# Projecting the first three channel chunks from x that has not been normalised yet, with x, weights and vectors laid out by the host

## The chip, the core and the metric

One NeuronCore of a Trainium2 chip runs the whole kernel. The metric is the device time of one execution in microseconds (us), the median of three runs. The engines are named as in the profile: PE (matrix products, with PEld for its weight loads), DVE (vector), ACT (scalar functions), POOL (GpSimd) and SP, which only issues DMAs here. Every engine works through its own instructions in the order in which the program holds them.

## What is computed

One layer over 1024 tokens with 1024 channels, all float32:

```
hn   = x * rsqrt(mean(x^2) + eps) * ln_g            # per token
proj = hn @ w_in + b_in                             # 1024 -> 3584 columns = 28 chunks of 128
glu_a, glu_b, z_conv, q, k, v, z_att = split(proj)  # 7 parts of 512 columns = 4 chunks each
u    = glu_a * sigmoid(glu_b)                       # then a convolution over tokens, 31 taps per channel
y_conv = pointwise(silu(layernorm(conv(u))))        # 512 x 512 product
y_att  = attention(q, k, v)                         # 8 heads, windows of a 16 x 64 token grid
out  = rms_norm(x + concat(norm(y_conv) * silu(z_conv), norm(y_att) * silu(z_att)) @ w_out) * final_g
```

Every factor of a matrix product is split into a rounded part and a remainder (`hi`, `lo` for the activations, `wh`, `wl` for the weights), and each product is three matmuls: hi.wh, lo.wh and hi.wl.

## The kernel before

**A planned order.** The function `block` runs on the host and writes the order of all engines by hand. A class `Clock` (L86 to 145) keeps a planned time for PE and for the queues of ACT, DVE and POOL, with a cost per instruction. The work is written as generators ("streams") with a rank. `weave` takes the first stream in rank order that is due, lets it emit instructions until it waits for a planned time, and goes on. A matmul moves the planned time forward. Two kinds of filler stand beside the streams: the taps of the convolution go to DVE whenever DVE's planned queue is empty to within 0.1 us, and the remainders `wl` of the weights go to POOL in the same way. The order is fixed once the program is built: where the chip is slower than the plan, the engines wait for each other in the planned order.

**Buffers.** `Ring` counts free buffers. `r_u` counts a pool of sixteen 4 KB-per-partition buffers in SBUF (the function `U`), which serve x, the tiles of `u`, q, k and v of a head pair, the attention outputs `ya`, and the pointwise weights. A stream that needs one takes it from `r_u` or polls until one is put back. Of the eight PSUM banks, tags `pj`, `s` and `tr` have two each and `o` and `ln` one each.

**The start.** SP loads the eight tiles of 128 tokens x 1024 channels (`xload`, L204), the weights of the first chunk after four of them, then small tensors. Per token tile, `x_tile` (L259) lets ACT (or DVE for tiles 4 and 6) square x and sum it, POOL makes 1/rms of the sum with two instructions (`rs`), and DVE scales the tile in place. `turned` (L279) lets PE transpose the scaled tiles in blocks of 128 x 128 (64 transposes, tile `px`) into PSUM banks of one channel block by 512 tokens; ACT copies each bank to `hi` with the scale `ln_g`, and `low` (L306) lets DVE write `lo` from the bank, the scale and `hi`. Tokens go in two halves, h = 0 and h = 1, of 512 each. The per-channel vectors and the taps arrive in rows and are turned by PE as well.

**The projection.** `prefetch` (L337) loads one weight chunk of 512 KB at a time on SP in 512-byte pieces (one raw buffer, `r_raw`), ACT writes `wh` in two halves, POOL writes `wl` in two halves; two chunks can be held (`r_w`). `proj` (L368) is 8 channel blocks x 3 matmuls of 512 columns into one bank, for one chunk and one token half. The stream `lead` runs `glu` for the pairs g0, g1, g2 (chunk b, then chunk a), then q0, k0 and v0; after it `attention` starts with rank 1 and `fill` (the rest of the projection) with rank 5. In `glu` (L505) a bank of chunk b leaves by ACT as a tanh (tile `sg`), one of chunk a by ACT with its bias, and DVE multiplies both (`glu_out`). When both halves are done, 31 taps for the chunk are queued as filler for DVE. For j = 0 the order is b h0, a h0, b h1, a h1; for j = 1 it is b h0, b h1, a h0, a h1.

**What else matters here.** `bias_rows` (L397) builds the bias of the attention through DRAM with some hundred small DMAs on SP, one per step of other work; attention starts when the first of it is there. Attention walks 32 blocks (4 head pairs of 8). A pair needs q (2 buffers), kh and kl (4), vt (1, put back when v is made) and v (2). `v_out` (L609) makes v; `head_out` takes one buffer for `ya` when a pair is done. `scores` gives back three buffers at the last block of a head. `pw_load` takes two buffers, and two more later, for the pointwise weights; then `pointwise` runs eight tiles of 128 tokens, each also waiting for its taps. Gates (`pz`), the last gates and the output projection (`out`) follow.

The change touches the start (`xload`, `x_tile`, `turned`, `low`, `tap_cols`), `prefetch`, `low_weight`, `proj`, `glu`, `glu_out` and the inputs that the host prepares.

Of the kernel before, what the change touches and what calls it, by code (L numbers as in the profile page):

```python
# [9 lines left out]
F32 = mybir.dt.float32  # L10
# [7 lines left out]
P = 128  # L18
# [35 lines left out]
TURN = 0.02  # L54
QI = 0.1
LW = 10.9
SQ_DVE = (4,6)

# [89 lines left out]
@with_exitstack  # L148
def block(ctx: ExitStack, tc: tile.TileContext, x, vecs, w_in, dw_w, pw_w, pw_b, rpb, w_out, final_g, out):
    nc = tc.nc  # L150
# [14 lines left out]
    ring = lambda n: Ring(ck, n)  # L165
    r_u, r_raw, r_w, r_x, r_uh, r_ul, r_gz, r_y = ring(16), ring(1), ring(2), ring(XB), ring(1), ring(0), ring(1), ring(1)
    r_pt, r_os = ring(2), ring(2)
# [5 lines left out]
    def U(name, dt=F32, shape=(P, 1024)):  # L173
        return big.tile(list(shape), dt, tag="u", name=name)
# [25 lines left out]
    acc = yp.tile([P, NC4, T], F32, name="acc")  # L200
    xt = [U(f"x{t}") for t in range(NT)]

    def xload(t):
        nc.sync.dma_start(out=xt[t], in_=x2[t * P:(t + 1) * P, :])  # L204

# [4 lines left out]
    def wraw(n):  # L210
        c = order[n]
        raw = wrp.tile([P, NK, P], F32, tag="wr", name=f"wr{c}")
        nc.sync.dma_start(out=raw, in_=w_in[0][:, c * P:(c + 1) * P].rearrange("(k p) n -> p k n", p=P))
        return raw

    def wtiles(n):
        c = order[n]
        return (whp.tile([P, NK, P], F32R, tag="wh", name=f"wh{c}"),
                wlp.tile([P, NK, P], F32R, tag="wl", name=f"wl{c}"))

    for t in range(4):
        xload(t)
    raw0 = wraw(0)
    for t in range(4, NT):
        xload(t)
    land = [4.5, 5.9, 7.4, 8.9, 11.8, 13.3, 14.7, 16.2]
    land_w = LW

    vec = half_tile("uh", "vec")[:V_N, :P]
    nc.scalar.dma_start(out=vec, in_=vecs)  # L230
    dwr = half_tile("ul", "dwr")[:TAPS, :C]
    nc.sync.dma_start(out=dwr, in_=dw_w[0])
    pwb = const.tile([P, C], F32, name="pwb")
    nc.sync.dma_start(out=pwb, in_=pw_b[0].partition_broadcast(P))

    cols = const.tile([P, V_N], F32, name="cols")
    pv = bank("tr", "pv")
    nc.tensor.transpose(out=pv[:, :V_N], in_=vec, identity=ident[:V_N, :V_N])
    nc.vector.tensor_copy(out=cols, in_=pv[:, :V_N])
# [4 lines left out]
    dwc = const.tile([P, NC4, 32], F32, name="dwc")  # L244

    def tap_cols():
        yield 19.0
        yield from r_tr.get()
        pd = bank("tr", "pd")
        for c in range(NC4):  # L250
            ck.tp(pd[:, c * 32:c * 32 + TAPS], dwr[:, c * P:(c + 1) * P], ident[:TAPS, :TAPS])
        t = ck.dve("tensor_scalar", out=dwc[:, :, :TAPS],
                   in0=pd[:, :NC4 * 32].rearrange("p (c k) -> p c k", k=32)[:, :, :TAPS], scalar1=0.5, scalar2=None,
                   op0=ALU.mult)
        r_tr.put(t)
        r_ul.put(t)
# [4 lines left out]
    x_ready, hn_ready = {}, {}  # L261

    def x_tile(t):
        yield land[t]
        ss = sm.tile([P, 1], F32, tag="ss", name=f"ss{t}")
        rs = sm.tile([P, 1], F32, tag="rs", name=f"rs{t}")
        eng = "dve" if t in SQ_DVE else "act"
        while t >= 4 and ck.q[eng] > ck.now + QI:
            yield ck.now + 0.1
        if t in SQ_DVE:  # L270
            e = ck.dve("scalar_tensor_tensor", out=acc[:, t % 4, :], in0=xt[t], scalar=1.0 / 1024.0, in1=xt[t],
                       op0=ALU.mult, op1=ALU.mult, accum_out=ss)
        else:
            e = ck.act(out=acc[:, t % 4, :], in_=xt[t], func=AF.Square, scale=1.0 / 32.0, accum_out=ss)
        yield e
        ck.gps("tensor_scalar", 0.2, e, out=rs, in0=ss, scalar1=EPS, scalar2=None, op0=ALU.add)
        e = ck.gps("tensor_tensor", 0.47, 0.0, out=rs, in0=rs, in1=mhalf[:, :1], op=ALU.pow)
        yield e
        x_ready[t] = ck.dve("tensor_scalar", e, 0.55, out=xt[t], in0=xt[t], scalar1=rs, scalar2=None, op0=ALU.mult)  # L279

    def turned(h):

        todo_ = list(range(NK))
        for group in ((("tr", "tr", "s", "s", "o", "ln"),) if h == 0 else ()) + (("tr",), ("s",)) * NK:
            ks, todo_ = todo_[:len(group)], todo_[len(group):]
            pts = []
            for k, tag in zip(ks, group):
                yield from RB[tag].get()
                pts.append((k, tag, bank(tag, f"px{h}_{k}", NB[tag])))
            for j in range(4):  # L290
                t = 4 * h + j
                while t not in x_ready:
                    yield ck.now + 0.1
                if x_ready[t] + ck.HOP > ck.now:
                    yield x_ready[t] + ck.HOP
                for k, tag, pt in pts:
                    ck.tp(pt[:, j * P:(j + 1) * P], xt[t][:, k * P:(k + 1) * P], ident)
                    if j == 3:
                        sl = slice(512 * h, 512 * h + 512)
                        e = ck.act(out=hi[k][:, sl], in_=pt, func=AF.Copy, scale=col(V_LN + k))  # L300
                        ck.spawn(low(h, k, pt, sl, e, RB[tag]), -1)
            yield
        for _ in range(4):
            r_u.put()

    def all_turned():  # L306
        for h in range(2):
            yield from turned(h)

    def low(h, k, pt, sl, t, r):  # L310
        yield t
        t = ck.dve("scalar_tensor_tensor", t, out=lo[k][:, sl], in0=pt, scalar=col(V_LN + k),
                   in1=hi[k][:, sl].bitcast(F32), op0=ALU.mult, op1=ALU.subtract)
        r.put(t)
        hn_ready[k, h] = t

    bias = []
# [6 lines left out]
    for b in sum(prob, []):  # L324
        nc.gpsimd.memset(b, 0.0)
    ck.q["pool"] = 5.0

# [9 lines left out]
    def prefetch():  # L337
        for n in range(len(order)):
            if n < W_AHEAD or "pw" in state:
                yield from r_raw.get()  # L340
                raw, end = (wraw(n), ck.now + 4.0) if n else (raw0, land_w)
                yield from r_w.get()
            else:
                yield from r_w.get()
                yield from r_raw.get()
                raw, end = wraw(n), ck.now + 4.0
            whi, wlo = wtiles(n)
            yield end
            for k0 in range(0, NK, KS):
                kk = slice(k0, k0 + KS)  # L350
                t = ck.act(out=whi[:, kk, :], in_=raw[:, kk, :], func=AF.Copy)
# [15 lines left out]

    def proj(w, h, name, order=None, tag="pj"):  # L368

# [9 lines left out]
        for k in range(NK):  # L379
            while (k, h) not in hn_ready or k >= len(wt):  # L380
                yield ck.now + 0.1
            if max(hn_ready[k, h], wt[k]) > ck.now:
                yield max(hn_ready[k, h], wt[k])
            ck.mm(pj, whi[:, k, :], tok(hi[k]), k == 0, False)
# [122 lines left out]
    def glu(j):  # L507
# [3 lines left out]
        for e, h in ((0, 0), (1, 0), (0, 1), (1, 1)) if j == 0 else ((0, 0), (0, 1), (1, 0), (1, 1)):  # L511
            c = (CH_B, CH_A)[e] + j
            ws[e] = yield from weight(c)
            pj, sl = yield from proj(ws[e], h, f"p{'ba'[e]}{j}_{h}")
            if e == 0:
                yield from r_x.get()
                sgs[h] = X(f"sg{j}_{h}")
                t = ck.act(out=sgs[h], in_=pj, func=AF.Tanh, scale=0.5, bias=hcol(V_BIN + c))
                r_pj.put(t)
            else:  # L520
                t = ck.act(out=uj[:, sl], in_=pj, func=AF.Identity, bias=col(V_BIN + c))
                r_pj.put(t)
                ck.spawn(glu_out(j, h, uj, sgs[h], t), -1)
            if h:
                r_w.put()
            yield

    def glu_out(j, h, uj, sg, t):
        yield t
# [454 lines left out]

    del r_u.free[8:]
    ck.taps = all_taps()
    for t in range(NT):
        ck.spawn(x_tile(t), -2 if t < 4 else 1)
    ck.spawn(all_turned(), 0)
    ck.spawn(tap_cols(), -1)  # L990
    ck.spawn(prefetch(), -1)
# [223 lines left out]
_VECS = ["ln_g", "b_in", "dw_b", "cln_g", "cln_b", "gn_conv_g", "gn_att_g"]  # L1215
_INS = ["x", "vecs", "w_in", "dw_w", "pw_w", "pw_b", "rpb", "w_out", "final_g"]

# [18 lines left out]
```

## Time and profile before

| | |
|---|---|
| median of 3 runs | 571.23 us (568.81 to 573.75) |
| profiled execution | 572.21 us |
| its span in the trace | 570.4 us |
| PE busy | 539.3 us, 95% of the span |
| DVE busy | 412.2 us, 72% |
| mean granted clock | 0.992 |

The span leaves 1.8 us of the execution's time outside. Rows of the trace are listed below; in them L127 is every matmul, L131 every transpose on PE, L136 every ACT, L140 every DVE and L144 every POOL instruction that the planner emits, so tiles tell them apart.

### The profile page before, as it was taken

To read this page: it belongs to the slowest core of one execution; us is meant where nothing else is said; L and a number is where in the kernel's file an instruction comes from. 1 tells how busy PE (TensorE), PEld (TensorE's weight loads), DVE (VectorE), ACT (ScalarE), POOL (GpSimd) and SP (SyncE) were. 2 spreads that over 40 slices of the span, in tenths; PEclk is the share of its full clock that TensorE was granted. 3 is DMA by queue.
4 is the path that set the end of the run, shared out by engine and by line. 5 is a ranking of instruction groups with operands and counts; after the bars stand their busy time and mean duration, and the time that the engine had idled before them with its cause. 6 is when DMAs were issued, how large, how long until landed. Compare 5 with 4: busy or idle time off the path is not lost.

```text
span 570.4 us, 7827 instructions
## 1 busy us (share of the span) xinstructions
PE 539.3 (95%) x2717; PEld 447.2 (78%) x2717; DVE 412.2 (72%) x665; ACT 260.1 (46%) x634; POOL 195.1 (34%) x176
## 2 busy tenths in 40 slices
PE   4999999898999998999997999999999999999995
PEld 3688888676888886888786788788888888888885
DVE  4747999987999979988999884667564365464232
ACT  6552221124555153655465645875665555253121
POOL 7513543232222343232525152542515552031121
PEclk9999999998999999999998999999999999999999
DMA  9413546663123442263241241101101470044221
GB/s 330 145 14 84 168 128 223 172 192 111 40 57 103 125 105 66 74 149 103 65 142 54 77 120 46 38 26 52 39 0 38 158 284 0 2 148 145 78 75 74
DMA packets 62331, 57.74 MB, mean 101 GB/s; under 512 B 9981, under 2 KB 51765, under 8 KB 62292
## 3 DMA queue, kind: packets, MB, share of 16 engines
q1 hardware_dynamic: 62222, 57.22, 33.6%
q8 instruction: 21, 0.34, 0.3%
q14 instruction: 18, 0.15, 0.1%
q10 hardware_dynamic: 70, 0.03, 0.0%
HBM read 36.58 MB, written 11.58 MB: 84 GB/s over the span
## 4 chain that ended last, share of the span: by engine, by line
PE 71%; DVE 17%; DMA 4%; issue 3%; ACT 2%; SPq 2%; POOL 1%; POOLq 0%; ACTq 0%; DVEq 0%
PE out L127 15%; PE pz L127 13%; DVE acc L140 12%; PE pv L127 6%; PE pk L127 6%; PE pq L127 5%; PE po L127 4%; PE pw L127 4%; PE pb L127 4%; PE ptp L131 3%; PE pa L127 3%; PE s L127 3%; DMA kl<-kl 1%; PE po L131 1%; DMA x<-in_x 1%
## 5 line engine op out<-in xcount | busy, mean ns | idle before, releaser
L140 DVE SCALAR_TENSOR_TENSOR acc<-glu,dwc,acc 128x512 f32<-128x512 f32 (+25 forms) x150 | 186.7, 1270 | 1.2
L144 POOL TENSOR_TENSOR wl<-wr,wh 128x512 fp32r<-128x512 f32 x56 | 93.9, 1695 | 153.0 <-ACT wh L136 147.7
L127 PE MATMUL pz<-hi,wh 128*128 128x512 f32 x128 | 52.2, 408 | 0.0
L127 PE MATMUL out<-wol,yh 128*128 128x512 f32 (+1 forms) x136 | 51.2, 377 | 0.0
L127 PE MATMUL out<-woh,yl 128*128 128x512 f32 (+1 forms) x136 | 51.2, 377 | 0.0
L127 PE MATMUL out<-woh,yh 128*128 128x512 f32 (+1 forms) x136 | 51.2, 377 | 0.0
L127 PE MATMUL pz<-hi,wl 128*128 128x512 f32 x128 | 50.3, 393 | 0.1
L127 PE MATMUL pz<-lo,wh 128*128 128x512 f32 x128 | 50.1, 391 | 0.0
L136 ACT ACTIVATE wh<-wr 128x512 fp32r<-128x512 f32 x56 | 32.3, 628 | 30.5 <-DMA wr<-in_w_in 20.9
L140 DVE TENSOR_TENSOR ptl<-ptp,pth 128x512 fp32r<-128x512 f32 x64 | 37.0, 614 | 1.2 <-ACT pth L136 1.2
L136 ACT ACTIVATE pth<-ptp 128x512 fp32r<-128x512 f32 x64 | 31.8, 543 | 13.2 <-PE ptp L131 12.4
L140 DVE CUSTOM_DVE_ANT_0 s<-s,bias 128x264 f32<-128x264 f32 (+1 forms) x64 | 30.2, 512 | 7.3 <-PE s L127 4.2
L140 DVE TENSOR_TENSOR xr<-out,xr 128x512 f32<-128x512 f32 (+1 forms) x17 | 11.1, 660 | 33.6 <-PE out L127 29.1
L136 ACT ACTIVATE prob<-s,mx 128x264 f32<-128x264 f32 (+1 forms) x64 | 33.6, 536 | 0.6 <-DVE mx L140 0.4
L136 ACT ACTIVATE os<-po 128x256 f32<-128x256 f32 x32 | 12.4, 387 | 41.9 <-PE po L127 41.8
L131 PE MATMUL ptp<-ident,prob 128*128 128x128 f32 x224 | 30.0, 273 | 0.0
L127 PE MATMUL pq<-hi,wh 128*128 128x512 f32 x64 | 26.6, 416 | 3.2 <-DVE v L140 3.2
L127 PE MATMUL po<-pth,v 128*128 128x256 f32 x112 | 29.5, 291 | 0.0
L144 POOL TENSOR_TENSOR ams<-ams,mhalf 128x8 f32<-128x8 f32 x8 | 14.6, 1819 | 43.5 <-DVE ams L140 43.5
L127 PE MATMUL po<-ptl,v 128*128 128x256 f32 x112 | 29.3, 290 | 0.0
L127 PEld LDWEIGHTS out<-woh,yh 128*128 128x128 f32 x136 | 25.6, 188 | 4.7
L127 PEld LDWEIGHTS out<-woh,yl 128*128 128x128 f32 x136 | 25.6, 188 | 4.7
(153 smaller groups left out, 1371.0 us busy)
## 6 DMA issues: line engine op xcount, KB each, us to landing
wr<-in_w_in SPq DMA_DIRECT2D x28, 512.0 KB
x<-in_x SPq DMA_DIRECT2D x8, 512.0 KB
wor<-in_w_out SPq DMA_DIRECT2D x8, 512.0 KB
xr<-in_x SPq DMA_DIRECT2D x8, 512.0 KB
out<-xr SPq DMA_DIRECT2D x16, 256.0 KB
kh<-kh SPq DMA_DIRECT2D x24, 128.0 KB
kl<-kl SPq DMA_DIRECT2D x24, 128.0 KB
q<-ql SPq DMA_DIRECT2D x16, 128.0 KB
```

Of the source, the lines that this page charges most:

```text
L127: self.nc.tensor.matmul(out, lhsT=lhsT, rhs=rhs, start=start, stop=stop)
L131: self.nc.tensor.transpose(out=out, in_=in_, identity=identity)
L136: self.nc.scalar.activation(**k)
L140: getattr(self.nc.vector, fn)(**k)
L144: getattr(self.nc.gpsimd, fn)(**k)
```

## The change

The host hands in x twice (by tokens, and by channels as `xt`), the weights in the order chunk, partition, channel block (so 4 KB in a row per partition), and the vectors and taps already by channels. The start then reads x by channels (`xc`, one tile per channel block) in 256 KB pieces, and makes `hi` and `lo` from `xc * ln_g` without 1/rms. The first three chunks (`RAW`: b of pair 0, a of pair 0, b of pair 1), both halves, are projected from these. x by tokens is loaded later, only for the sums of squares; 1/rms is broadcast over the partitions by a PE transpose (`stats`) into `rsb`. The six banks of the three chunks are multiplied by `rsb` on DVE as they leave PSUM, and `normalise` then scales `xc` in place and writes `hi` and `lo` anew for the other 25 chunks. Six buffers of `r_u` are free at the start instead of eight: `xc` has eight, the second raw weight chunk one, `rsb` one. The diff, without the signature, the load-time constants and the parts of `glu` that only move:

```
+RAW = ((0, 0), (1, 0), (0, 1))
-    xt = [U(f"x{t}") for t in range(NT)]
+    xc = [U(f"xc{k}") for k in range(NK)]
+    def xload(k0, n, h):
+        for k in range(k0, k0 + n):
+            nc.sync.dma_start(out=xc[k][:, 512 * h:512 * h + 512], in_=xt[k][:, 512 * h:512 * h + 512])
+    def tload(t):
+        nc.sync.dma_start(out=acc[:, t % 4, :], in_=x2[t * P:(t + 1) * P, :])
...
-        nc.sync.dma_start(out=raw, in_=w_in[0][:, c * P:(c + 1) * P].rearrange("(k p) n -> p k n", p=P))
+        nc.sync.dma_start(out=raw, in_=w_in[c])
...
+    raws0 = [wrp.tile([P, NK, P], F32, tag="wr", name=f"wr{order[0]}"), U(f"wr{order[1]}", F32, (P, NK, P))]
+    for h in range(2):
+        for k in range(NK):
+            first(("x", k, h), 0.25, xload, k, 1, h)
+            if h == 0 and k in (0, 3):
+                first(("w", 0, (k + 1) // 4), 0.25, wload, 0, 4 * (k // 3), 4)
+        if h == 0:
+            first(("w", 1, 0), 0.5, wload, 1, 0, NK)
     for t in range(4):
+        first(("t", t), 0.5, tload, t)
...
+    rsb = U("rsb")
+    def x_raw(k, h):
+        yield land["x", k, h]
+        sl = slice(512 * h, 512 * h + 512)
+        t = ck.act(out=hi[k][:, sl], in_=xc[k][:, sl], func=AF.Copy, scale=col(V_LN + k))
+        yield t
+        raw_ready[k, h] = ck.dve("scalar_tensor_tensor", t, out=lo[k][:, sl], in0=xc[k][:, sl], scalar=col(V_LN + k),
+                                 in1=hi[k][:, sl].bitcast(F32), op0=ALU.mult, op1=ALU.subtract)
+    def stats():
+        for h in range(2):
+            tag = ("o", "ln")[h]
+            yield from RB[tag].get()
+            pb = bank(tag, f"rsb{h}", NB[tag])
+            for j in range(4):
+                t = 4 * h + j
+                yield land["t", t]
...
+                e = ck.act(out=acc[:, j, :], in_=acc[:, j, :], func=AF.Square, scale=1.0 / 32.0, accum_out=ss)
+                if h == 0:
+                    tload(t + 4)
...
+                ck.tp(pb[:, j * P:(j + 1) * P], rs.broadcast_to([P, P]), ident)
+            e = ck.act(out=rsb[:, 512 * h:512 * h + 512], in_=pb, func=AF.Copy)
...
+    def normalise(h):
+        while h not in raw_done or h not in rs_ready:
+            yield ck.now + 0.1
+        yield rs_ready[h]
+        sl = slice(512 * h, 512 * h + 512)
+        for k in range(NK):
+            t = ck.dve("scalar_tensor_tensor", out=xc[k][:, sl], in0=xc[k][:, sl], scalar=col(V_LN + k), in1=rsb[:, sl],
+                       op0=ALU.mult, op1=ALU.mult)
+            ck.spawn(split_x(k, h, sl, t), -1)
+            yield
+    def split_x(k, h, sl, t):
+        yield t
+        t = ck.act(t, out=hi[k][:, sl], in_=xc[k][:, sl], func=AF.Copy)
+        yield t
+        q = dict(out=lo[k][:, sl], in0=xc[k][:, sl], in1=hi[k][:, sl].bitcast(F32), op=ALU.subtract)
+        t = ck.gps("tensor_tensor", 1.4, t, **q) if k % 2 else ck.dve("tensor_tensor", t, **q)
         hn_ready[k, h] = t
+        if h:
+            r_u.put(t)
...
-            r_raw.put(t)
+            (r_u if n == 1 else r_raw).put(t)
...
+            if (e, j) in RAW:
+                tag = ("pj", "s", "tr")[h if j == 0 else 2]
+                pj, sl = yield from proj(ws[e], h, f"p{'ba'[e]}{j}_{h}", None, tag, raw_ready)
+                if (e, j) == RAW[-1]:
+                    raw_done[h] = True
+                ck.spawn((raw_a if e else raw_b)(j, h, c, uj, sgs, pj, sl, RB[tag]), -1)
...
+    def raw_a(j, h, c, uj, sgs, pj, sl, banks):
...
+        t = ck.dve("tensor_tensor", out=uj[:, sl], in0=pj, in1=rsb[:, sl], op=ALU.mult)
+        banks.put(t)
+        yield t
+        t = ck.act(t, out=uj[:, sl], in_=uj[:, sl], func=AF.Identity, bias=col(V_BIN + c))
+        yield from glu_out(j, h, uj, sgs, t)
...
-    del r_u.free[8:]
+    del r_u.free[6:]
```

`raw_b` does the same with tanh for chunk b. `x_tile`, `turned`, `low` and `tap_cols` are gone, and with them the 64 transposes and those of the vectors and taps. `rsb` is never put back to `r_u`.

## Rows read from the trace of the kernel before

**Rows 1.** Page, busy time of the engines over the span.
```profile
PE 539.3 (95%) x2717; PEld 447.2 (78%) x2717; DVE 412.2 (72%) x665; ACT 260.1 (46%) x634; POOL 195.1 (34%) x176
```

**Rows 2.** Stages: from:to, length, busy PE, PEld, DVE, ACT, POOL, granted clock, DMA share, GB/s.
```profile
0.00:46.80 46.80, 37.60 (x173) 29.50 (x174) 24.20 (x34) 23.82 (x40) 22.04 (x41) 1.00 0.50 160
125.60:277.80 152.20, 145.58 (x783) 121.03 (x781) 135.19 (x227) 75.25 (x196) 45.30 (x25) 0.99 0.35 93
277.80:307.50 29.70, 26.68 (x152) 22.75 (x152) 28.43 (x54) 16.05 (x43) 8.89 (x6) 1.00 0.41 118
307.50:341.90 34.40, 32.18 (x166) 26.88 (x167) 29.50 (x54) 18.86 (x48) 13.57 (x14) 0.95 0.31 80
341.90:447.60 105.70, 104.68 (x584) 88.31 (x584) 60.40 (x134) 66.00 (x175) 44.88 (x40) 1.00 0.11 33
```

**Rows 3.** Chain that ended last, in order of time: start, length, what.
```profile
2.11 7.01 DMA x<-in_x
39.88 5.45 PE pa L127 x24
```

**Rows 4.** Groups of instructions in 0 to 46 us: count, busy, mean ns, idle before.
```profile
L131 PE MATMUL px<-ident,x 128*128 128x128 f32 x64 | 12.5, 345 | 3.9 <-DVE x L140 3.9
```

**Rows 5.** Order of time, PE, 16 to 19 us: start, length, line, what.
```profile
17.46 0.63 PE L127 MATMUL pb<-lo,wh 128*128 128x512 f32 x1
17.88 0.63 PE L127 MATMUL pb<-hi,wl 128*128 128x512 f32 x1
```

**Rows 6.** Order of time, ACT, 55 to 69 us.
```profile
56.24 0.69 ACT L136 ACTIVATE sg<-pb,hcols 128x512 f32<-128x512 f32 x1 [4.75 <-PE pb L127]
67.12 0.69 ACT L136 ACTIVATE glu<-pa,cols 128x512 f32<-128x512 f32 x1 [4.75 <-PE pa L127]
```

**Rows 7.** The chain again, 45 to 73 us.
```profile
56.02 1.28 DVE acc L140
58.64 2.19 DVE acc L140
```

**Rows 8.** Order of time, POOL, 0 to 64 us.
```profile
11.62 3.93 POOL L144 TENSOR_TENSOR wl<-wr,wh 128x512 fp32r<-128x512 f32 x2 [0.19 <-ACT wh L136]
58.13 1.62 POOL L144 TENSOR_TENSOR wl<-wr,wh 128x512 fp32r<-128x512 f32 x1 [5.83 <-ACT wh L136]
```

**Rows 9.** Order of time, DVE, around 14 us and from 260 us.
```profile
14.36 2.72 DVE L140 SCALAR_TENSOR_TENSOR lo<-px,cols,hi 128x512 fp32r<-128x512 f32 x4
...
262.67 0.74 DVE L140 SCALAR_TENSOR_TENSOR acc<-glu,dwc,acc 128x512 f32<-128x512 f32 x1
278.38 0.54 DVE L140 TENSOR_SCALAR acc<-glu,dwc,cols 128x512 f32<-128x512 f32 x1
340.39 1.50 DVE L140 SCALAR_TENSOR_TENSOR acc<-glu,dwc,acc 128x498 f32<-128x498 f32 x2
```

**Rows 10.** Groups of DVE instructions by shape.
```profile
L140 DVE TENSOR_TENSOR xn<-pw,pwb 128x512 f32<-128x512 f32 x8 | 5.5, 692 | 24.4 <-PE pw L127 24.4
L140 DVE TENSOR_TENSOR ul<-xn,uh 128x512 fp32r<-128x512 f32 x8 | 5.5, 683 | 3.2 <-ACT uh L136 3.2
```

**Rows 11.** Stages again, around the stall at 305 us.
```profile
305.00:307.50 2.50, 0.29 (x2) 0.00 (x0) 2.46 (x10) 2.39 (x8) 0.52 (x1) 1.00 0.35 105
307.50:312.00 4.50, 3.97 (x20) 3.67 (x21) 4.40 (x11) 3.04 (x9) 2.88 (x4) 0.62 0.00 0
```

**Rows 12.** Order of time, PE, 265 to 276 us.
```profile
268.99 0.41 PE L127 MATMUL pv<-hi,wl 128*128 128x512 f32 x1
270.66 0.60 PE L131 MATMUL pvt<-ident,vt 128*128 128x128 f32 x4
273.24 1.04 PE L131 MATMUL yat<-ident,ytok 128*128 128x128 f32 x8
274.12 0.60 PE L131 MATMUL pvt<-ident,vt 128*128 128x128 f32 x4
```

**Rows 13.** Order of time, SP's DMA issues, 255 to 310 us.
```profile
295.99 0.37 SPq L826 DMA_DIRECT2D pwr<-in_pw_w  x1
```

More of the change, by code (lines that the diff above doesn't have):

```diff
@@ L243, in block @@
     hcol = lambda r: hcols[:, r:r + 1]
[L244 to L256, printed above, removed]
+    nc.vector.tensor_scalar(out=dwc, in0=dwc, scalar1=0.5, scalar2=None, op0=ALU.mult)
@@ L281, in turned @@
[L281 to L289, printed above, removed]
+    raw_ready, hn_ready, rs_ready, raw_done = {}, {}, {}, {}
+    rsb = U("rsb")
[6 more added lines that the diff above has]
+                                 in1=hi[k][:, sl].bitcast(F32), op0=ALU.mult, op1=ALU.subtract)
@@ L302, in turned @@
-            yield
[L303 to L310, printed above, removed]
+                yield land["t", t]
+                ss = sm.tile([P, 1], F32, tag="ss", name=f"ss{t}")
+                rs = sm.tile([P, 1], F32, tag="rs", name=f"rs{t}")
+                e = ck.act(out=acc[:, j, :], in_=acc[:, j, :], func=AF.Square, scale=1.0 / 32.0, accum_out=ss)
+                if h == 0:
+                    tload(t + 4)
+                    land["t", t + 4] = max(land.get(("t", t + 3), 0.0), e + 3.0) + 1.5
@@ L339, in prefetch @@
             if n < W_AHEAD or "pw" in state:
-                yield from r_raw.get()
-                raw, end = (wraw(n), ck.now + 4.0) if n else (raw0, land_w)
+                if n != 1:
+                    yield from r_raw.get()
+                raw, end = (wraw(n), ck.now + 4.0) if n > 1 else (raws0[n], 0.0)
                 yield from r_w.get()
@@ L379, in proj @@
         for k in range(NK):
-            while (k, h) not in hn_ready or k >= len(wt):
+            while (k, h) not in x_ready or k >= len(wt):
                 yield ck.now + 0.1
-            if max(hn_ready[k, h], wt[k]) > ck.now:
-                yield max(hn_ready[k, h], wt[k])
+            if max(x_ready[k, h], wt[k]) > ck.now:
+                yield max(x_ready[k, h], wt[k])
             ck.mm(pj, whi[:, k, :], tok(hi[k]), k == 0, False)
@@ L526, in glu, with raw_b, glu_out @@
             yield
-    def glu_out(j, h, uj, sg, t):
+    def raw_b(j, h, c, uj, sgs, pj, sl, banks):
+        while h not in rs_ready:
+            yield ck.now + 0.1
+        yield rs_ready[h]
+        yield from r_x.get()
+        sg = X(f"sg{j}_{h}")
+        t = ck.dve("tensor_tensor", out=sg, in0=pj, in1=rsb[:, sl], op=ALU.mult)
+        banks.put(t)
+        yield t
+        ck.act(t, out=sg, in_=sg, func=AF.Tanh, scale=0.5, bias=hcol(V_BIN + c))
+        sgs[h] = sg
+    def raw_a(j, h, c, uj, sgs, pj, sl, banks):
+        while h not in rs_ready:
+            yield ck.now + 0.1
+        yield rs_ready[h]
+        t = ck.dve("tensor_tensor", out=uj[:, sl], in0=pj, in1=rsb[:, sl], op=ALU.mult)
+        banks.put(t)
+        yield t
+        t = ck.act(t, out=uj[:, sl], in_=uj[:, sl], func=AF.Identity, bias=col(V_BIN + c))
+        yield from glu_out(j, h, uj, sgs, t)
+    def glu_out(j, h, uj, sgs, t):
+        while h not in sgs:
+            yield ck.now + 0.1
+        sg = sgs[h]
         yield t
@@ L983, in lead @@
         state["lead"] = True
-    del r_u.free[8:]
+    del r_u.free[6:]
     ck.taps = all_taps()
[L987 to L990, printed above, removed]
+    for h in range(2):
+        for k in range(NK):
+            ck.spawn(x_raw(k, h), -2)
+        ck.spawn(normalise(h), -1)
+    ck.spawn(stats(), -1)
     ck.spawn(prefetch(), -1)
@@ L1224 @@
     nc = bacc.Bacc("TRN2", target_bir_lowering=False, num_devices=1)
-    inputs = dict(inputs, vecs=np.concatenate([np.asarray(inputs[n])[0].reshape(-1, P) for n in _VECS]))
+    a = {n: np.asarray(v) for n, v in inputs.items()}
+    inputs = dict(
+        a,
+        xt=a["x"][0].T.reshape(NK, P, T),
+        vecs=np.concatenate([a[n][0].reshape(-1, P) for n in _VECS]).T,
+        w_in=a["w_in"][0].reshape(NK, P, -1, P).transpose(2, 1, 0, 3),
+        taps=np.pad(a["dw_w"][0], ((0, 1), (0, 0))).reshape(32, NC4, P).transpose(2, 1, 0))
     arrays, args = {}, []
```

99 lines of the change are left out of this document (35 added, 64 removed).

## The prediction

> **What bounds the kernel now.** I read the page's busy times first, then the chain that ended last, then stage windows, then the order of time at the start and wherever the change's buffers and waits come into play. PE is busy for 95% of the span, DVE for 72% [rows 1]: the kernel is bound by PE wherever PE is fed. The windows say where it is not. Up to 46.8 us PE is busy for 37.6 us, but a good part of that is transposes of x and matmuls at half clock: 64 transposes take 12.5 us, with 3.9 us of waiting for the scaled x before them [rows 4]; matmuls start 0.42 us apart at 17.5 us [rows 5], against 5.45 us for a projection of 24, or 0.227 us each, at 40 us [rows 3]. [...] The two token halves of b and a of pair 0 end at 45.3 us; four projections at full pace need 4 x 5.45 = 21.8 us, so the start costs 23.5 us. From 341.9 to 447.6 us PE is busy for 104.7 of 105.7 us [rows 2]; there is nothing to win there but work.
>
> So time gained at the start is kept if later waits don't take it back. Two could. DVE is full from 47 us on: it works 135 of 152 us up to 277.8 us, and 28.4 of the next 29.7 [rows 2], the taps filling what the rest leaves. And the sixteen buffers of `r_u` gate the later stages: the second load of pointwise weights is issued at 295.99 us [rows 13], when the fourth block of a head gives three buffers back.
>
> **The start, step by step.** The change ends the wait for the norm. SP's burst grows from 8 x loads, one weight chunk and three small loads to 16 pieces of x, 3 of weights, 4 tiles of x by tokens and two small loads, about 7.3 MB before the other four x tiles. The first four tiles, 2.1 MB, landed 7.0 us after 2.1 us [rows 3], 300 GB/s with the latency in it. So x of the first half with chunk b (2.6 MB) is there by 2.1 + 8.7 = 10.8 us, and the first four token tiles by 26 us at the latest. DVE's eight `lo` set the pace of the first projection: from about 5.3 us to 14.2 at 1.1 us each, the middle of 0.74 and 1.37 (worked out below). Add the last three matmuls, and it ends at 14.9 us; at the half-clock pace all the way 24 x 0.427 from 5 us give 15.2, so the clock changes little here. Three more projections end at 14.9 + 16.4 = 31.3 us. The eight broadcasts of 1/rms are transposes like those removed, at most 12.5/64 = 0.2 us each: 1 us. So b and a of pair 0 end at 32.2 us and b of pair 1, two more, at 43.1 us. Before, the same point is where ACT takes the second bank of b at 56.24 us [rows 6], so PE is 13 us ahead there. The loads of x by tokens cost nothing, since 1/rms is wanted only when banks run short, at 43 us; the bias DMAs behind them on SP slip by the few microseconds of the four late loads, which attention doesn't see, as `fill` can run until the bias is there.
>
> **The price: `hi` and `lo` a second time.** `normalise(h)` may start when the raw chunks have read that half: at 37.7 us for h = 0. Per half, DVE multiplies a bank (0.69 us [rows 10]), does eight SCALAR_TENSOR_TENSOR on two SBUF operands and four subtractions (0.68 [rows 10]); POOL does four subtractions, ACT eight copies. All eight multiplications are emitted before the first subtraction, so a of pair 1 waits for the ninth instruction.
>
> What one such multiplication takes isn't in the trace; a tap of 512 columns is the nearest, also with two SBUF operands: 0.74 us alone [rows 9]. A tap of 1024 takes 1.28 us alone and 2.19 while POOL writes a `wl` [rows 7], which is there at 58.13 [rows 8]. The factor is 1.71, so 0.74 becomes 1.27, and up to 1.37 with the hops. `lo` from PSUM shows no such loss: four took 2.72 us, 0.68 each [rows 9], while POOL wrote two `wl` [rows 8]; the change moves that operand into SBUF too.
>
> Lower bound, POOL never in the way: 37.7 + 0.7 + 8 x 0.74 + 0.7 = 45.0 us. PE waits 1.9 us and ends the first half of a at 50.4; DVE ends the three other subtractions at 47.0, then the other half's bank, eight multiplications and one subtraction at 54.3; PE waits 3.9 us and ends at 59.7. Upper bound, POOL always in the way and a tap of 2.2 us in front: 51.6, 58.8 (with 1.7 us lost to half clock, below) and 75.5. Before, the point is 66.9 us, just before ACT takes the bank at 67.12 [rows 6]. So the 13 us become anything from a gain of 7.2 to a loss of 8.6 us. POOL has 8 subtractions and two `wl` to do, some 12.7 us at 1.27, against 22 us of DVE work, and so is in the way of about half of it: I take the middle, +0.5 us.
>
> The half clock after a wait: after 2.2 us of idle PE at 305 us the granted clock was 0.62 for 4.5 us [rows 11], so 4.5 x 0.38 = 1.7 us lost. A wait as short as the lower bound's first may cost nothing.
>
> [...]
>
> **What the rest does.** DVE's taps resume at about 62 us instead of running from 46.8 us, and start a little earlier; they are some 13 to 15 us behind. That lies beside PE's work: the first token half of the last chunk has its taps at 278.4 us, the second at 341.9 [rows 9], while the pointwise weights arrive only after 296 us [rows 13] and the last four tiles start far later. If the taps were over 18 us late, this cover would be gone.
>
> `r_u` has fifteen buffers in place of sixteen, as `rsb` keeps one. By my count of takes and puts from the code, all sixteen are held at one place, around 270 us: `u` 1, `ya` 1, q, k and vt of pair 2 7, pointwise 2, q of pair 3 2, v 2, the next `ya` 1. There the trace has the last matmul of v at 268.99, the transposes for v at 270.66 and 274.12, and those for `ya` between them at 273.24 us [rows 12]. With fifteen, `ya` must wait until vt is put back, so it moves from 273.2 to about 275.5, and with it the next pair's first block. PE holds q of pair 3 in the meantime, so the cost is from 0 to 3 us; I take 2. Weights in 4 KB pieces instead of 512 bytes cost or give nothing, as PE never waits for them after the start.
>
> **Sum.** 572.2 (profiled) + 0.5 + 2 = 574.7 us. The profiled execution lay 1.0 us above the median, so 573.7; I say 573.5 us. Its own range is 567 to 580.
>
> **Rivals.**
> 1. *The gain survives.* If POOL's subtractions hardly meet DVE's, the lower bound holds: 571.2 - 7.2 = 564 us if the wait for the buffer is hidden, 566 if it isn't. For it: ACT has to make `hi` before POOL can start, so POOL's work lags. Against it: `wl` of two chunks are due in the same stretch.
> 2. *DVE and POOL in turn.* 18.8 + 12.7 = 31.5 us from 37.7 us end the last `lo` at 69.2 us; with the last matmuls and the half clock after a long wait a ends at about 72 us, 5 us late. With the taps late too, 571.2 + 5 + 2 + 2 = 580 us. It decides from the point at which the wait before the second half of a passes 7 us.
> 3. *The fifteenth buffer locks.* In the order of time on PE, v's takes come about 1 us before `ya`'s (268.99 against 273.24 less some 3.2 us of POOL work and hops). If `ya` takes its buffer first, v gets one and holds it; the next to come free is that of the last `u`, after its taps, at about 312 us when DVE has only taps to do and they are 13 us late. Attention stands for 35 us; PE has the rest of q and one gate, 21 us, and then idles for about 21. Price 16 to 35 us, so about 593 us. It decides from a shift of 1 us between the two.
> 4. *The loads are too slow*, so that x by channels, not DVE, paces the start: 2.6 MB at 300 GB/s ends 3.4 us before DVE does, so little is left for this; time as before.
>
> **How the numbers follow.** Forecast 0.38, first rival 0.30, second 0.17, third 0.13, fourth 0.02. A measurement of this kernel tells about 1%, or 5.7 us, from no change. Faster: 0.29 of the first. Same: 0.35 of the forecast, 0.01 each of the first two rivals, 0.02 of the fourth. Slower: 0.03 of the forecast, 0.16 of the second, 0.13 of the third. The range 561 to 592 leaves out the best of the first rival and the worse part of the third.
>
> **What would show it.** Right: b of pair 1 is through PE by 43 us, with two waits of PE on DVE's `lo` right behind it, 2 to 8 us each, and a of pair 1 ends near 67 us; multiplications near 0.74 us alone and 1.3 us beside POOL; the first taps run for a moment before 38 us and then from about 62 us; `ya` of pair 1 behind the second v transpose. Wrong: a of pair 1 ending before 61 us; attention standing for over 10 us near 270 or 360 us; the pointwise tiles waiting for taps.

## The result, and the profile after

The changed kernel takes 624.49 us (622.14 to 625.09), against 571.88 us (568.81 to 573.75) for the kernel before measured beside it: a ratio of 1.092, with an interval of 1.086 to 1.098. That is slower by 52.6 us and outside the range of the prediction. Pairs are counted from 0 here, as in the prediction. (Some expectations below call the first pair "pair 1": "v of pair 1" that ends the lead is v of pair 0, and pvt "of pair 3" and "of pair 4" are those of pairs 2 and 3.)

The page first, beside [rows 1]: PE's busy time is almost the same, its span is not.

```profile
PE 543.6 (87%) x2656; PEld 448.1 (72%) x2656; DVE 427.5 (69%) x682; ACT 274.4 (44%) x656; POOL 209.2 (34%) x184
```

The same five stages as in [rows 2] (from:to, length, busy PE, PEld, DVE, ACT, POOL, granted clock, DMA share, GB/s). In the fourth PE works 9.76 of 34.4 us, where it had 32.18, and at a granted clock of 0.57.

```profile
0.00:46.80 46.80, 37.68 (x147) 29.68 (x147) 23.60 (x29) 29.13 (x48) 22.78 (x41) 0.96 0.76 250
125.60:277.80 152.20, 149.07 (x790) 124.08 (x789) 138.86 (x227) 72.16 (x188) 44.93 (x24) 0.99 0.35 96
277.80:307.50 29.70, 21.25 (x101) 16.83 (x99) 29.42 (x27) 9.31 (x19) 14.82 (x9) 0.93 0.27 80
307.50:341.90 34.40, 9.76 (x44) 7.72 (x44) 27.58 (x48) 5.06 (x15) 0.00 (x0) 0.57 0.08 25
341.90:447.60 105.70, 99.60 (x552) 83.86 (x553) 57.51 (x135) 67.49 (x179) 39.13 (x38) 0.98 0.19 53
```

PE's waits of the whole run (waiting line, what released it: total, times, longest):

```profile
PE po L126 <- DVE v L139: 29.8, 1, 29.8
PE pa L126 <- DVE lo L139: 11.5, 2, 9.2
...
PE pz L126 <- POOL wl L143: 5.5, 1, 5.5
```

PE in order of time, the ends that the prediction named and the long wait. The lines of before for `yat` and `pvt` are [rows 12].

```profile
25.97 0.32 PE L130 MATMUL rsb<-ident,rs 128*128 128x128 f32 x1 [1.99 <-POOL rs L143]
...
47.90 0.39 PE L126 MATMUL pb<-hi,wl 128*128 128x512 f32 x1
...
55.65 0.27 PE L130 MATMUL rsb<-ident,rs 128*128 128x128 f32 x1
...
68.93 0.79 PE L126 MATMUL pa<-lo,wh 128*128 128x512 f32 x1 [9.16 <-DVE lo L139]
...
76.62 0.39 PE L126 MATMUL pa<-hi,wl 128*128 128x512 f32 x1
...
295.82 1.03 PE L130 MATMUL yat<-ident,ytok 128*128 128x128 f32 x8
296.70 0.60 PE L130 MATMUL pvt<-ident,vt 128*128 128x128 f32 x4
297.60 0.66 PE L130 MATMUL pvt<-ident,vt 128*128 128x128 f32 x4 [0.30 <-DVE ya L139]
298.58 1.17 PE L130 MATMUL ptp<-ident,prob 128*128 128x128 f32 x6 [0.32 <-ACT ya L135]
329.50 0.55 PE L126 MATMUL po<-pth,v 128*128 128x256 f32 x1 [29.75 <-DVE v L139]
```

PE stands for 29.8 us because v of pair 2 isn't written, though its transposes are through PE by about 298 us. DVE in order of time says why, and what the start looks like:

```profile
40.65 8.50 DVE L139 SCALAR_TENSOR_TENSOR xc<-xc,cols,rsb 128x512 f32<-128x512 f32 x8
49.08 0.68 DVE L139 TENSOR_TENSOR sg<-pb,rsb 128x512 f32<-128x512 f32 x1
49.68 4.05 DVE L139 TENSOR_TENSOR lo<-xc,hi 128x512 fp32r<-128x512 f32 x4
56.59 8.99 DVE L139 SCALAR_TENSOR_TENSOR xc<-xc,cols,rsb 128x512 f32<-128x512 f32 x8 [2.86 <-ACT rsb L135]
...
68.06 2.63 DVE L139 TENSOR_TENSOR lo<-xc,hi 128x512 fp32r<-128x512 f32 x4
...
71.92 0.81 DVE L139 TENSOR_SCALAR acc<-glu,dwc,cols 128x1024 f32<-128x1024 f32 x1
...
293.75 3.11 DVE L139 SCALAR_TENSOR_TENSOR acc<-glu,dwc,acc 128x1010 f32<-128x1010 f32 x3
...
303.70 25.31 DVE L139 SCALAR_TENSOR_TENSOR acc<-glu,dwc,acc 128x512 f32<-128x512 f32 x30
328.94 1.41 DVE L139 TENSOR_TENSOR v<-pvt,v 128x256 fp32r<-128x256 f32 x4
```

Thirty taps of the last `u` run back to back, and directly behind them v is written: v had to wait for the buffer that the last `u` gives back. The first tap starts at 71.92 us; before, it was 46.81. The last 1024-wide tap (the end of the third `u`) ends at 296.9 us; before, at 248.1, as the second of two taps that one row of DVE's order of time holds:

```profile
246.16 1.92 DVE L140 SCALAR_TENSOR_TENSOR acc<-glu,dwc,acc 128x510 f32<-128x510 f32 x2
```

ACT and POOL in the start show where 1/rms was late:

```profile
30.49 1.15 ACT L135 ACTIVATE wh<-wr 128x512 fp32r<-128x512 f32 x2 [6.94 <-PE pb L126]
31.55 1.04 ACT L135 ACTIVATE acc<-acc 128x1024 f32<-128x1024 f32 x1
...
37.15 0.60 ACT L135 ACTIVATE rsb<-rsb 128x512 f32<-128x512 f32 x1 [4.47 <-PE rsb L130]
...
55.95 0.60 ACT L135 ACTIVATE rsb<-rsb 128x512 f32<-128x512 f32 x1 [4.41 <-PE rsb L130]
```

```profile
24.60 0.35 POOL L143 TENSOR_SCALAR rp<-rp 120x31 f32<-120x31 f32 x1 [8.12 <-DMA rp<-in_rpb]
25.03 0.23 POOL L143 TENSOR_SCALAR rs<-ss 128x1 f32<-128x1 f32 x1
...
47.19 4.79 POOL L143 TENSOR_TENSOR lo<-xc,hi 128x512 fp32r<-128x512 f32 x3
52.05 0.55 POOL L143 TENSOR_SCALAR rs<-ss 128x1 f32<-128x1 f32 x1
```

The first 1/rms stands on POOL behind `rp`, a small instruction for the bias of the attention that waits 8.12 us for its DMA. The fourth square stands on ACT behind a `wh` that waits 6.94 us for PE to let its buffer go; the last 1/rms stands on POOL behind three subtractions.

### The profile page after: what moved, and what is told of

It is laid out like the page before. It is cut to its first block, busy times and chain, and to the rows that moved or that the text cites. A ratio compares the mean times of both kernels' runs of the same rounds, so it can differ in the third digit from the quotient of the medians.

```text
span 622.9 us, 7800 instructions
## 1 busy us (share of the span) xinstructions
PE 543.6 (87%) x2656; PEld 448.1 (72%) x2656; DVE 427.5 (69%) x682; ACT 274.4 (44%) x656; POOL 209.2 (34%) x184
## 5 line engine op out<-in xcount | busy, mean ns | idle before, releaser
L139 DVE SCALAR_TENSOR_TENSOR acc<-glu,dwc,acc 128x512 f32<-128x512 f32 (+25 forms) x150 | 180.9, 1237 | 1.2
L126 PE MATMUL po<-pth,v 128*128 128x256 f32 x112 | 30.2, 294 | 30.6 <-DVE v L139 29.8
L135 ACT ACTIVATE wh<-wr 128x512 fp32r<-128x512 f32 x56 | 32.3, 628 | 33.4 <-DMA wr<-in_w_in 15.7
L126 PEld LDWEIGHTS po<-pth,v 128*128 128x128 f32 x112 | 21.7, 194 | 32.8 <-issue 30.0
L126 PE MATMUL pa<-lo,wh 128*128 128x512 f32 x64 | 27.0, 423 | 11.5 <-DVE lo L139 11.5
L139 DVE TENSOR_TENSOR ytok<-po,ytok 128x128 f32<-128x128 f32 x32 | 9.2, 288 | 35.6 <-ACT ytok L135 35.0
L126 PE MATMUL pb<-hi,wh 128*128 128x512 f32 x64 | 27.7, 433 | 6.0 <-ACT wh L135 6.0
L126 PEld LDWEIGHTS pz<-hi,wl 128*128 128x128 f32 x128 | 24.6, 192 | 11.4 <-POOL wl L143 5.9
```

The source lines that it names most:

```text
L126: self.nc.tensor.matmul(out, lhsT=lhsT, rhs=rhs, start=start, stop=stop)
L135: self.nc.scalar.activation(**k)
L139: getattr(self.nc.vector, fn)(**k)
```

## The experiments

All medians are beside runs of the kernel before on the same chip (570.96 to 572.12 us). The table holds what decided: the start of the first full run of taps, the end of the last 1024-wide tap, the end of the lead (last matmul of v of pair 0), how many of the 93 wide taps of the first three `u` had not started then, and the start of the second `pvt` of pairs 2 and 3. Times are in us, from the order of time of each trace; where PE's work ends, the start of its last matmul is given. In e9, e10 and e12 the first tap stands alone, some 4 us ahead of the next; in e11 a single tap ran at 45.4 us.

| run | first tap | third u's taps end | lead ends | wide taps left | pvt pair 2 | pvt pair 3 | median |
|---|---|---|---|---|---|---|---|
| before | 46.8 | 248.1 | 125.4 | 42 | 274.1 | 362.0 | 571.88 |
| after | 71.9 | 296.9 | 133.9 | 54 | 297.6 | 407.3 | 624.49 |
| e1, after, 16 buffers | 71.8 | 304.1 | 133.9 | 54 | 276.5 | 390.9 | 598.34 |
| e2, before, 15 buffers | 45.1 | 245.5 | 123.7 | 42 | 296.0 | 389.9 | 609.07 |
| e3, e1 and sums first | 69.7 | 302.6 | 130.3 | 54 | 275.0 | 389.2 | 593.18 |
| e4, e1 with two raw chunks | 70.1 | 279.7 | 141.8 | 47 | 285.3 | 374.3 | 585.65 |
| e5, after, v asks first | 72.4 | 298.0 | 134.8 | 54 | 298.7 | 387.9 | 596.93 |
| e6, before, taps late | 69.2 | 301.2 | 122.9 | 59 | 291.8 | 386.3 | 591.14 |
| e7, e3 and e4 together | 60.5 | 271.7 | 133.0 | 47 | 277.3 | 364.6 | 576.47 |
| e9, e7, lo on DVE | 50.2 | 256.8 | 127.4 | 46 | 269.2 | 357.6 | 569.19 |
| e10, e3, lo on DVE | 61.3 | 296.7 | 125.9 | 54 | 269.1 | 383.2 | 589.83 |
| e11, before, taps 14 us late | 61.6 | 280.3 | 120.9 | 53 | 283.4 | 369.9 | 593.04 |
| e12, e7, order alone | 55.2 | 262.6 | 134.0 | 45 | 275.2 | 362.9 | 572.02 |

**The buffer.** e1 gives `rsb` back after the last of its seven readers; e2 takes one buffer from the kernel before.

```
-    rsb = U("rsb")
+    rsb, rsb_left = U("rsb"), [7]
+    def rsb_read(t):
+        rsb_left[0] -= 1
+        if not rsb_left[0]:
+            r_u.put(t)
```

> The change, with the buffer of rsb put back to r_u after its last reader (16 buffers in the long run instead of 15). Theory A (the lock on the buffers at pair 2 costs most): the wait of 29.8 us of PE on v at 300 us goes, the second load of pointwise weights is issued near 300 us instead of 337, and the time falls by 35 to 45 us, to 580 to 590. Theory B (the taps, some 25 us late, hold the buffer of the second u and make the shortage by themselves): PE still waits over 15 us for v of pair 2 and the time stays above 605.

```
-    del r_u.free[8:]
+    del r_u.free[7:]
```

> The kernel before with one buffer of r_u taken away and nothing else. Theory A: v of pair 2 gets one buffer and waits for the second until the taps of the last u are done; a wait of PE on v of 15 to 35 us appears between 270 and 330 us, and the time rises from 572 to 595 to 615. Theory B: the start and the taps are as before, so the time stays within 1% of 572.

e1: 598.34 us, ratio 1.048 (1.043 to 1.054). The wait of 29.8 us is gone and `pvt` of pair 2 is back at 276.5 us; 26 us are won, not 35 to 45, since pair 3 now is late (390.9 against 362.0 us). e2: 609.07 us, 1.066 (1.061 to 1.071), with nothing of the start changed, and with the wait of the changed kernel, half as long, behind a `pvt` that is 22 us late:

```profile
312.06 0.55 PE L127 MATMUL po<-pth,v 128*128 128x256 f32 x1 [14.75 <-DVE v L140]
```

So the missing buffer alone costs 38 us in the kernel before, and giving it back wins 26 us in the changed one. But 27 us stay.

**The order of asking.** e5 keeps 15 buffers and only lets `ya` ask later, and not while a v still lacks one of its two:

```
     def v_out(i, vt, t):
+        v_left[0] += 2
         for _ in range(2):
             yield from r_u.get()
+            v_left[0] -= 1
...
-        yield from r_u.get()
         yield t + PEA
+        while v_left[0]:
+            yield ck.now + 0.1
+        yield from r_u.get()
```

> The changed kernel with its 15 buffers as they are, and only the order of asking changed: ya of a pair is asked for after its head's output is ready, and not while a v of the next pair still wants one of its two. Theory A (the 30 us wait of pair 2 is the order of asking, a lock between ya and the second v buffer): the wait for v at 329.5 us goes, pvt of pair 3 is transposed near 285-292 us instead of 297, and the time falls by 20 to 35 us to 590-605 us, with 15 buffers and late taps as before. Rival B (one buffer too few holds something in any order, the taps set the end): within 8 us of 624, 616 to 632. Rival C (the start sets the time): 620 to 630.

596.93 us, 1.045 (1.042 to 1.047): the order alone wins 27.6 us without a buffer. PE's wait for v is 2.0 us instead of 29.8, although `pvt` starts no earlier (298.7 us, a miss of the expectation). So it was no lack of room as such: v of pair 2 held one buffer, `ya` took the next, and the one after that was the last `u`'s.

**The start.** e3 and e4 begin from e1. e3 computes all eight sums and 1/rms in a stream of their own, ahead of the broadcasts; e4 has two raw chunks instead of three; e7 has both.

```
+    def sums():
+        for t in range(NT):
...
+            e = ck.act(out=acc[:, j, :], in_=acc[:, j, :], func=AF.Square, scale=1.0 / 32.0, accum_out=ss)
...
+            rss[t] = rss[t], e
...
+    ck.spawn(sums(), -1)
```

> As e1, and all eight sums of squares and 1/rms are made without a PE broadcast between them; the broadcasts follow in two groups of four. Theory F (the sums wait for PE, since each broadcast stands in PE's order between projections and ACT's next square behind ACT's copies): rsb of the second half is there by 45 us instead of 56, PE's 9.2 us wait before the second half of a of pair 1 falls below 5, the end of that chunk moves from 76.6 to 68 to 72 us, and the time is 3 to 8 below e1. Theory G (DVE's multiplications beside POOL set that wait): rsb comes earlier, but the chunk ends within 2 us of 76.6 and the time is within 2 us of e1.

```
-RAW = ((0, 0), (1, 0), (0, 1))
+RAW = ((0, 0), (1, 0))
```

> As e1, with only the first two chunks projected from x without its norm, so that normalise of the first half may run beside the projections of the second half. Theory F: as 1/rms is the late one, the first wait grows, because the next chunk wants it 11 us earlier; the start ends no earlier and the time is 0 to 8 above e1. Theory G: the multiplications are hidden, the start ends 4 to 8 us earlier than in e1, and so does the kernel.

> The change with two raw chunks instead of three, all sums and 1/rms ahead of the other work of the start, and rsb given back after its last reader (16 buffers). Theory A (what stays is the start: later lead, no lock): the lead's last v ends 130 to 138 us against 125.4, no wait of over 5 us for v later, time 576 to 584 us, 2 to 9 below the 585.65 of two chunks alone. Rival B (the lock of pair 3 comes back when the start moves by a few us): 590 to 600 us. Rival C (the saved start is worth its whole, ahead of the kernel before): 564 to 570 us.

e3: 593.18 us. The copy of the second half's `rsb` starts at 39.02 us instead of 55.95, yet a of pair 1 ends at 74.66 instead of 76.62, and PE still waits 6.0 us before its second half: the late 1/rms was real, and hid that the normalise step behind it was as late by itself. e4: 585.65 us, 1.024 (1.020 to 1.029). Neither expectation holds: its lead ends 8 us later than that of e1 and its time is 12.7 us shorter. When the lead ends, 47 wide taps are left instead of 54; the third `u` is done at 280 us instead of 304, and v of pair 3 waits less. So the start doesn't set the time by itself. e7: 576.47 us, 1.009 (1.006 to 1.011), without a long wait for v; its lead is still 7.7 us late.

**Late taps alone.** e6 and e11 are the kernel before, with all taps held back until a planned time (65 for e6, 57 for e11):

```
+TLATE = 65.0
...
-            live = todo[:2]
+            live = todo[:2] if ck.now > TLATE else []
```

> The kernel before with nothing changed but that no tap is queued on DVE until about 25 us later than now (first one near 70 us instead of 46.8); x, projection, 16 buffers as before. Theory A (late taps alone hold u's buffers longer, so that v of the fourth pair gets its second buffer only from the last u): the projections of the lead end as in the kernel before (v of pair 1 ends within 2 us of 125.4), the wait of pair 3 appears (pvt near 380-392 us instead of 358), and the time is 583 to 600 us. Rival B (the late start of the projection costs the time, the taps have 18 us of room and more): 568 to 577 us.

> The kernel before, its taps held back so that the first is queued some 14 us later (near 61 us instead of 46.8), nothing else. The prediction's own step (13 to 15 us are covered, there were 18 us of room): 569 to 575 us, and the last 1024-wide tap of the third u ends 14 us later, at 255 to 260 us instead of 243. Theory A (what is not done in the lead, where DVE makes taps back to back, is made up at half that rate beside the attention, so lateness about doubles): the last 1024-wide tap ends at 265 to 285 us, and the time is 574 to 592 us, the more the nearer it comes to 290 us.

e6: 591.14 us, 1.035 (1.032 to 1.038), with a lead that ends 2.5 us *earlier* than before. e11: 593.04 us, 1.038 (1.034 to 1.043). In DVE's order of time the last 1024-wide taps stand at

```profile
292.40 8.82 DVE L141 SCALAR_TENSOR_TENSOR acc<-glu,dwc,acc 128x1012 f32<-128x1012 f32 x7
```

in e6, and in e11 at

```profile
279.08 3.50 DVE L141 SCALAR_TENSOR_TENSOR acc<-glu,dwc,acc 128x1009 f32<-128x1009 f32 x4
```

Of these four only the first is wide; it ends at 280.3 us. The 243 us in the expectation of e11 is where an earlier wide tap of the kernel before ends; its last ends at 248.1. So 22 us late at the start are 53 us late at the third `u` in e6; 15 us are 32 us in e11. In the kernel before, 30 taps run on DVE from 80 to 125 us, 0.67 per us, and 24 from 120 to 180 us, 0.40 per us, where the attention has begun. What the lead leaves undone is made up at the slower pace. The table shows it in every run: from the end of the lead to the end of the third `u` it is 2.8 to 3.2 us per wide tap left. What counts for the third `u` is thus how many taps the lead leaves, not when the first one starts, as e4 beside e1 shows. The time of e6 holds a wait of PE for v of its own, 9.8 us up to 302.9 us; DVE writes that v at 302.4 us, right behind the third `u`. e11 ends just above the 574 to 592 us of its theory A and, less late than e6, isn't faster: beside the later v it waits 8.5 us for weights of a gate near 470 us (2.48 for `wh`, 6.01 for `wl`; none of these before). So lateness doesn't have one price per microsecond; that the planned order puts the gates elsewhere when taps are late would explain e11, but wasn't tested.

**The normalise step.** e9 (two raw chunks) and e10 (three) make every `lo` of the normalised x on DVE, each one multiplication behind its own; e12 changes the order alone and leaves POOL its half.

```
             ck.spawn(split_x(k, h, sl, t), -1)
...
-            yield
+            yield t
...
-        t = ck.gps("tensor_tensor", 1.4, t, **q) if k % 2 else ck.dve("tensor_tensor", t, **q)
+        t = ck.dve("tensor_tensor", t, **q)
```

> The run with two raw chunks and the sums first, with all subtractions for lo of the normalised x on DVE, each right behind the multiplication after its own, instead of half of them on POOL and the others behind all eight multiplications. Theory P (POOL beside DVE and the place in DVE's order set the normalise step): the eight multiplications of the second half cost 0.75 to 0.9 us each instead of 1.45, the wait of PE for lo (8.75 us) falls under 4 us, v of pair 1 ends 125 to 130 us instead of 133, time 568 to 574 us. Rival Q (the late 1/rms sets it, wherever lo is made): v of pair 1 within 2 us of 133, time 574.5 to 578.5 us.

> The run with three raw chunks, the buffer given back and the sums first, with all subtractions for lo of the normalised x on DVE, each right behind the multiplication after its own. Theory P on the start: PE's waits for lo (6.5 and 6.0 us) fall to under 5 us together, a of pair 1 ends 62 to 68 us (74.7 there, 66.9 before the change), v of pair 1 ends 118 to 125 us. On the time, theory A (the taps decide, they still start 10 us or more later than before the change, and the third u's taps end after 285 us): pvt of pair 4 after 378 us and 580 to 592 us though the start is as good as before the change or better. Rival R (a good start brings the gain the change was made for): 562 to 571 us.

> The run with two raw chunks and the sums first, where only the order on DVE changes: a subtraction for lo stands behind the multiplication after its own instead of behind all eight; POOL keeps its half of the subtractions. It parts the two halves of what the run with all subtractions on DVE changed together. Theory P1 (POOL beside DVE is the price): the multiplications of the second half stay at 1.2 to 1.5 us each, v of pair 1 ends 130 to 134 us, time 573 to 578 us. Rival P2 (the place in the order is the price): DVE's waits behind eight multiplications go, v of pair 1 ends 126 to 129 us, time 567 to 572 us.

In e7, which e9 and e12 start from, DVE's order of time shows eight multiplications of the first half at 0.80 us and of the second, beside POOL's subtractions and two `wl`, at 1.45 us each:

```profile
31.01 6.44 DVE L139 SCALAR_TENSOR_TENSOR xc<-xc,cols,rsb 128x512 f32<-128x512 f32 x8 [8.89 <-ACT rsb L135]
...
42.98 11.60 DVE L139 SCALAR_TENSOR_TENSOR xc<-xc,cols,rsb 128x512 f32<-128x512 f32 x8 [1.93 <-ACT rsb L135]
```

In e9 all of the second half take 0.74 us, as here:

```profile
50.93 0.74 DVE L139 SCALAR_TENSOR_TENSOR xc<-xc,cols,rsb 128x512 f32<-128x512 f32 x1
51.59 1.28 DVE L139 TENSOR_TENSOR lo<-xc,hi 128x512 fp32r<-128x512 f32 x2
```

e9 takes 569.19 us, 0.997 (0.994 to 0.999): 1.9 us below the kernel before, the fastest of all here, though within 1%. Its lead ends 5.7 us earlier than in e7. PE's waits for `lo` didn't fall (9.2 us against 8.75, a miss), but they came in ten pieces of at most 2.1 us, and the granted clock from 33 to 66 us was 0.90 instead of 0.74. DVE is busy for 32.25 of those 33 us, so it has hardly any room left there. e12, with the order alone: lead at 134.0 us, as P1 said, and 572.02 us, 1.000 (0.999 to 1.002), at the edge between the two expectations. P1's other sign is missed: of the eight multiplications of the second half seven took 0.74 us and one 1.76. PE waits 4.3 us for `lo` from DVE and 4.0 us for `lo` from POOL. So POOL's half of the subtractions is what delays the lead, by 6.6 us beside e9, but not by slow multiplications alone; POOL's own `lo` come late too. With the new order the taps start 5 us earlier than in e7, and the time is 4.5 us shorter.

e10 shows the third raw chunk with the best start that was found: a of pair 1 ends at 68.13 us (66.69 before the change), the lead at 125.9 us (125.4 before), so nothing is won there, and both lie just above the ranges of theory P (68 and 125); the taps start 14.5 us later, and the time is 589.83 us, 1.033 (1.029 to 1.037), as theory A said. `normalise` overwrites x, so a third raw chunk puts it off: the first multiplication is at 40.09 us, in e9 at 29.51.

**Layout alone.** e8 is the kernel before with `w_in` laid out by the host (`in_=w_in[c]`).

> The kernel before with one part of the change alone: w_in laid out by the host so that a chunk of 128 columns is one piece of 4 KB per partition. Theory A (weights land ahead of their use, the layout buys nothing): 568 to 574 us, the page's packets fall by some 20000. Rival B (fewer packets free the queues and shorten the exchange loads of q and k): 560 to 567 us.

572.16 us, 1.001 (0.998 to 1.004): no difference, as predicted. The vectors and taps turned by the host were not run by themselves.

## Why the prediction was wrong

Point by point, by its own steps.

- **PE's lead at b of pair 1.** Predicted 43.1 us, measured 47.9 (before, ACT took that bank at 56.24 [rows 6]). The broadcasts of 1/rms stand between PE's matmuls: one waited 1.99 us before 25.97 us, and the granted clock from 21.1 to 30.3 us was 0.81. About 5 of the 13 us were gone. The first projection ended at 15.7 us, not 14.9. The 0.427 us per matmul that the prediction sets beside it stand in no row of before; the changed kernel shows them, with starts 0.427 us apart from 8.52 to 12.36 us. But what the prediction calls half clock at the start is half the pace: the record's granted clock is 1.00 there, from 8 to 12 us as in [rows 2]; 0.50 goes with the same pace from 26.9 to 29.9 us.
- **"The loads of x by tokens cost nothing, since 1/rms is wanted only at 43 us."** This step failed. The loads were in time (three squares are done by 23.5 us), the chain behind them was not: ACT, POOL and PE each had it behind other work, and the second half's `rsb` was there at 56 us. The prediction let the bias DMAs slip because attention wouldn't see it, but the first 1/rms did: it stood on POOL behind `rp` until 25.03 us, 4 us after its square. e3 keeps that order (its `rp` is at 24.89 us) and moves the rest of the chain; this is worth only 2 us of PE's time at that point, 5 us of the whole.
- **The normalise step.** The multiplications took 1.06 and 1.12 us, in the middle of the predicted 0.74 to 1.37 (of which 0.1 us for hops was the author's estimate). But a of pair 1 ended at 76.6 us, beyond the upper bound of 75.5, because that bound let the second half start without a late 1/rms; in e3, without one, it ends at 74.7. (The middle of the two bounds is 0.7 us, not the 0.5 of the sum, which changes nothing.) The two waits of PE came, 2.4 and 9.2 us.
- **The taps: 13 to 15 us late, covered up to 18, so nothing in the sum.** This step failed. They were 25 us late; e6 shows 22 us to cost 19 us in the kernel before, and e11 that even 15 us cost 22 us, 8.5 of which stand at the weights of a gate. The prediction counted the lateness as constant and looked for its cover at the pointwise tiles. It grew to more than twice its size (22 us became 53 in e6, 15 became 32 in e11) once DVE shared its time with the attention, and it was felt earlier, through the buffers that the `u` hold.
- **Fifteen buffers, taken at +2 us.** This is the term of the sum that was furthest off: 27.6 us in e5 instead of 2. The third rival came, given 0.13: v holding one, `ya` taking the next, the last `u`'s taps ending the wait. Its account was right (wait 29.8 us; price 16 to 35, measured 26.2 in e1 and 27.6 in e5); the choice between the two was not. It hung on 1 us of order that the prediction itself named, with a price of 16 to 35 us on one side, and the start had moved by far more than 1 us.

The sum as the runs show it: about 27 us from the order of asking with 15 buffers (e5), 19 us from late taps (e6, in the kernel before), together 46 of 52.6 us. The rest, some 6 us, fits the lead that ends 8.5 us later, but wasn't measured by itself. The parts needn't add up: e6's 19 us hold a wait for v of 9.8 us, so both have to do with the same buffers.

The first rival, that the gain survives, isn't borne out with three raw chunks even in e10. Of the second, DVE and POOL in turn, some waits are there. In e12, DVE and POOL in order of time:

```profile
48.61 1.76 DVE L139 SCALAR_TENSOR_TENSOR xc<-xc,cols,rsb 128x512 f32<-128x512 f32 x1
...
58.78 2.29 DVE L139 SCALAR_TENSOR_TENSOR acc<-glu,dwc,acc 128x1009 f32<-128x1009 f32 x1
```

```profile
48.00 1.82 POOL L143 TENSOR_TENSOR wl<-wr,wh 128x512 fp32r<-128x512 f32 x1
...
58.33 1.67 POOL L143 TENSOR_TENSOR lo<-xc,hi 128x512 fp32r<-128x512 f32 x1 [1.95 <-ACT hi L135]
```

The multiplication of 0.74 us ends 0.55 us after POOL's instruction (50.37 against 49.82), the tap of 1.28 us ends 1.07 us after it (61.07 against 60.00). That is the whole instruction but for 0.2 us, behind POOL's end, in both. The same holds in the kernel before: the tap at 58.64 us [rows 7] ends at 60.83, 1.08 us after the `wl` that ends at 59.75 [rows 8]. So 2.19 was the tap behind what was *left* (1.11 us) of an instruction already running, and the prediction's factor of 1.71 is that of this one pair. That all work of the two engines stands one behind the other, as the second rival adds it up (18.8 us for DVE's part, 2 x (0.7 + 8 x 0.74 + 4 x 0.7), and 12.7 for POOL's), the runs don't show: seven of the eight multiplications of the second half took 0.74 us in e12. From four `lo` with one operand in PSUM, 0.68 us each, the prediction read that these don't lose; only the first two of them stood beside POOL's `wl` (up to 15.55 us [rows 8]). The changed kernel has one more such case: the bank's multiplication at 49.08 us took 0.68 us beside POOL's subtractions of 47.19 to 51.98 us.

## What to carry to other kernels

Where a filler (here the taps) gives back buffers, its lateness must be followed to the buffers, by the work that is left undone and at the pace at which it can be made up there, not compared with the slack of its last reader. Where two streams take from one pool that is exhausted at one point, and a stream needs two at once, the order of asking is worth as much as a buffer: if a microsecond decides it, a shift of the start decides it anew, and the forecast should follow the worse side. And work moved to an engine that is full in that stretch (DVE here, 98% busy from 33 to 66 us in e9) can leave the waits as long in all: PE's for `lo` were 9.2 us there and 8.75 in e7, though the lead ended 5.7 us earlier.

## What the runs showed of the hardware that was not expected

- In the three pairs above, a DVE instruction with two SBUF operands behind a running POOL instruction took all that was left of POOL's and then its own length less 0.2 us: 0.74 became 1.76 us and 1.28 became 2.29 in e12, 1.28 became 2.19 in the kernel before. It isn't so of every one: in e12 a `lo` from two SBUF operands began at 48.01 us, 0.01 us after POOL's `wl`, and took 0.68 us. On the mean of eight multiplications, 0.80 became 1.45 us in e7.
- The length of PE's waits alone doesn't tell what they cost in clock. A wait of 2.12 us that ended at 220.56 us in the kernel before was followed by a granted clock of 1.00 (220.5 to 226 us), one of 2.12 us that ended at 223.35 us in the changed kernel by 0.69 (223.3 to 227 us). From 33 to 66 us the granted clock was 0.74 in e7, with one wait of 8.75 us and PE still for 15.1 of the 33 us; 0.90 in e9, with waits of at most 2.1 us and PE still for 10.4 us; but 0.79 in e12, with waits of at most 1.4 us and PE still for 10.7 us. What parts e9 from e12 stays open.
